# A decoder layer's output projection as seven block products, and transposes taken some turns later

## The chip, the cores and the metric

The kernel runs on one core of a Trainium2 chip. Its engines work side by side, each through its own list of instructions: TensorE (PE) multiplies matrices into PSUM banks, VectorE (DVE) and ScalarE (ACT) work elementwise, GpSimd (POOL) does a few small operations and issues DMA transfers that add into what is in memory, and SyncE (SP) issues the other DMA transfers. The metric is the device time of one execution in microseconds (us).

## The reference

One layer of a decoder on 512 tokens of width 1024, in float32. The part that matters here:

```python
x = x + (gate_r * ret_branch + gate_a * att_branch) @ w_o      # w_o: 1024 x 1024
u = rmsnorm(x, g_mlp) @ w_up                                   # w_up: 1024 x 4096
x = x + jnp.square(jax.nn.relu(u)) @ w_down                    # w_down: 4096 x 1024
gate_p = jax.nn.sigmoid(rmsnorm(x, g_ple) @ w_ple_gate)
return x + gate_p * (p_i @ w_ple_proj)
```

Ahead of it stand one input projection, a retention branch and an attention branch of three head groups. `gate_r` and `gate_a` are sigmoids of two column ranges of the input projection, and `ret_branch` and `att_branch` are each a product with a weight matrix.

## The kernel before

**Three products for one.** Every large matrix product keeps float32 accuracy by splitting both sides into a high and a low part in the matmul format (`fp32r`) and adding three products: high by high, high by low, low by high (`mm3`, lines 260 to 262). Weights come from HBM in units of 512 KB (`raw`, six buffers) and are split (`split_unit`): ScalarE copies the high part (`whi`, line 227), VectorE subtracts to get the low part (`wlo`, line 228), with four buffers each. `AHEAD` says how many units beyond the current ones are split in advance.

**Projections.** `rows_gemm` puts tokens on the output's rows: four banks of 128 tokens x 512 columns. `cols_gemm` puts output columns on the rows and all 512 tokens in the bank's columns.

**The mix of the branches (`mix`).** For each block of 256 output columns, and for the attention branch and then the retention branch, a `cols_gemm` makes the gate and another the branch product. VectorE multiplies the two (`gt`, line 899), GpSimd adds the branches (`gm`, line 905), ScalarE and VectorE split the sum into `mh` and `ml`. The blocks go in the order 0, 1, then 2, 3.

**The output projection (`tail`, first part).** The token rows `x` are loaded, and two `rows_gemm` calls (left and right 512 columns) multiply the 1024 merged columns by `w_o`. As each bank of 128 tokens finishes, VectorE adds it to `x` (line 1020), multiplies by the gain (line 383), and some turns later TensorE transposes the result (`pt`, line 336; `split_T`) into the left side of the next product, `h2`, which is split again (lines 349 and 350). ScalarE's squares of the row give its norm factor.

**The MLP.** It goes in four rounds of 1024 hidden columns. A round's up projection is eight `cols_gemm` calls. Its down projection is already done as seven block products instead of eight (`seven_gemm`): both sides are taken as 2 x 2 blocks (tokens by 256, columns by 512), sums and differences of blocks are formed, and seven products of them give the four output blocks. `seven_left` forms the left factors on VectorE and splits them (lines 932 to 940). The right factors are formed as the weights are loaded: `plan_seven` lists fourteen units, eight of which are a load on SP and then an accumulating load on POOL into the same buffer (line 196); two units are differences taken on VectorE (line 209). The products are traced in the order 4, 3, 5, 2, 1, 7, 6, and after each the accumulations into `x` (line 967), with `done` telling when an output block of 128 tokens x 512 columns is complete.

**What sets the order.** Work that is due later is put in a queue with a number of turns (`later`), and `tick` takes at most one ready item, the first in the list, at each turn; in a `rows_gemm` of 1024 columns a turn comes after every six matmuls. The head transposes (`heads_T`), the attention's value products and the transposes of normed rows get their place in TensorE's list this way. The planner of the language then orders each engine's list by its own estimate of when operands are ready, and hoists loads to where their buffers come free. Only in the last round's down projection and in the gate projection behind it do ScalarE and VectorE keep the order in which the program was traced (`manual_schedule`), with `AHEAD` 3 in that down projection.

In the last round `seven_gemm` calls `ready` for each complete block: the transposes for `h3` are put in the queue, and when a row has both halves its squares are traced at once (`mean_squares`, lines 391 to 394). The embedding rows `pp` (two loads of 1 MB) are traced ahead of that down projection. `big` is a pool of 16 buffers of 8 KB per partition, which holds `x1`, the left factors, `h2`, `h3`, `z` and `pp` among others.

Of the kernel before, what the change touches and what calls it, by code (L numbers as in the profile page):

```python
# [11 lines left out]
F32 = mybir.dt.float32  # L12
# [63 lines left out]
class Block:  # L76
# [504 lines left out]
    def att_proj(self, g, n):  # L581
# [24 lines left out]
        else:  # L606
            self.rows_gemm(self.hT, KD, consume)
        return self.heads_T(rots, g > 0, 12)

# [30 lines left out]
    def attention(self, g):  # L640
# [11 lines left out]
        def scores(r):  # L652
# [17 lines left out]
            for e in es:  # L670
                self.later(8, lambda e=e: pTs.append(self.transpose4(e)))
            self.later(13, lambda: values(r, wide, pTs), ("att", g, r))

# [105 lines left out]
    def ret_proj(self, extra=None):  # L779
        rots = []  # L780

        def consume(t, ps):
            z = self.tmp("rz")
            self.nc.scalar.activation(z, ps, AF.Copy, scale=self.r[:, t : t + 1])
            rots.append(self.rotate(z, self.rc[:, 1, t, :HD], self.rc[:, 1, t, HD:]))
            if extra is not None:
                extra(t, rots[t])

        self.rows_gemm(self.hT, KD, consume)
        return self.heads_T(rots, False, 7)  # L790

# [40 lines left out]
    def ret_head(self, h, qk, v, G, inner, A):  # L832
# [43 lines left out]
        for i in range(NT):  # L876
            self.later(2, lambda i=i: values(i))


    def mix(self, A, O):  # L880
        nc = self.nc
        mx = self.new_act(2, "m")
        self.spread_factors()
        for c in range(0, 4, 2):
            parts = {}
            for br, act, nk, bo in (("a", O, H, 24), ("r", A, KD, 16)):
                for cc in (c, c + 1):
                    sg = []
# [8 lines left out]
                    def branch(n, ps):  # L897
# [3 lines left out]
                        if br == "a":  # L901
                            parts[kk] = t
                            return
                        m = self.tmp("gm")
                        nc.gpsimd.tensor_tensor(m, t, parts[kk], op=ALU.add)
                        hi, lo = mx[0][kk // 4][:, kk % 4], mx[1][kk // 4][:, kk % 4]
                        nc.scalar.activation(R(hi), m, AF.Copy)
                        nc.vector.tensor_tensor(R(lo), m, hi, op=ALU.subtract)

# [7 lines left out]
                    self.cols_gemm(act, nk, branch)  # L917
        return mx

    def plan_mix(self):  # L920
        for c in range(0, 4, 2):
            for gate, w, nk in ((GA, self.a["w_att_out"][0], H), (GR, self.a["w_ret_out"][0], KD)):
                for cc in (c, c + 1):
                    self.plan_cols(self.w_in, gate + 256 * cc, KD)
                    self.plan_cols(w, 256 * cc, nk)
# [16 lines left out]
    def seven_gemm(self, U, xs, f, ready):  # L942
# [51 lines left out]
        for p in range(2):  # L994
            nc.vector.tensor_tensor(m4[p], m4[p], banks[1, p], op=ALU.add)
            acc(0, 0, p, m4[p])
            acc(1, 1, p, m4[p])
        for u in range(2):
            product(7, 5, u, False, u == 1)
# [10 lines left out]
    def tail(self, mx):  # L1010
        nc, a = self.nc, self.a
        xb = [self.big("x1") for _ in range(2)]
        xs = [xb[t // 2].rearrange("p (t c) n -> p t (c n)", t=2)[:, t % 2] for t in range(NT)]
        for t in range(NT):
            nc.sync.dma_start(xs[t], a["x"][0, t * P : (t + 1) * P])

        def add(half):
            def f(t, ps):
                v = xs[t][:, half * 512 : (half + 1) * 512]
                nc.vector.tensor_tensor(v, v, ps, op=ALU.add)  # L1020
            return f

        g2 = self.gain_row("g_mlp")
# [4 lines left out]

        def first(t, ps):
            add(0)(t, ps)  # L1030
            self.gain_T(xs[t], t, 0, g2, h2, "h2", 5)

        def last(t, ps):
            add(1)(t, ps)
            self.gain_T(xs[t], t, 1, g2, h2, "h2", 3)
            self.mean_squares(xs[t], v2[:, t : t + 1])

        self.rows_gemm(mx, KD, first)
        self.rows_gemm(mx, KD, last, group=4)
        nc.vector.reciprocal(f2[:, :NT], v2)  # L1040
        nc.vector.tensor_scalar(f2[:, NT:], f2[:, :NT], -1.0, None, op0=ALU.mult)

        h3 = None
        for f in range(NF // 2):
# [17 lines left out]
            for jj in range(2):  # L1062
                if f == 0 and jj == 0:
                    self.cols_gemm_halves(h2, KD, lambda n, ps: act(n // 2, n % 2, ps),
                                          lambda t: self.force(("h2", t, 1)))
                else:
                    for b in range(2):
                        self.cols_gemm(h2, KD, lambda n, ps: act(b, 2 * jj + n, ps))
            if f == NF // 2 - 1:
                pp = [self.big("pp") for _ in range(2)]  # L1070
                for half in range(2):
                    nc.sync.dma_start(pp[half], self.pp_dram[:, 512 * half : 512 * (half + 1)].rearrange(
                        "(t p) n -> p t n", p=P))
            ready = None
            if f == NF // 2 - 1:
# [3 lines left out]
                def ready(t, j, free):  # L1079
# [4 lines left out]
                    if halves[t] == 2:  # L1084
                        v = self.small(1, "v")
                        self.mean_squares(xs[t], v)
                        nc.gpsimd.tensor_tensor(r3[:, t : t + 1], v, self.mhalf[:, :1], op=ALU.pow)
            if f == NF // 2 - 1:
# [4 lines left out]

        self.AHEAD = 2
        out = self.a["out"][0]
# [15 lines left out]
    def make_plan(self):  # L1111
# [9 lines left out]
        self.plan_mix()  # L1121
        for half in range(2):
            self.plan_rows(a["w_o"][0], 512 * half, KD)
        for f in range(NF // 2):
# [50 lines left out]
```

## Time and profile before

| | us |
|---|---|
| median of 3 runs | 1014.93 (1014.62 to 1015.85) |
| the profiled execution | 1015.35 |
| its span | 1013.6 |
| output projection (first to last matmul) | 581.0 to 627.9 |
| four rounds of the MLP | 627.9 to 964.0 |
| weight loads of `w_o`, each | 512 KB, 3.3 from issue to landing |
| accumulating loads of `w_down`, each | 512 KB, 7.2 from issue to landing |

The span counts from the first to the last instruction that was recorded; the execution's own time is 1.75 us longer. In the profile's groups a line is that of the helper that issued the instruction, so tiles tell more than lines: `pg` and `pb` are product banks, `ph` a bank of head transposes, `pt` a bank of transposed rows, `hh` and `hl` the input's left side, `h2h` and `h2l` the MLP's, `h3h` and `h3l` the last gate's, `uh` and `ul` the left factors of the seven products, `raw` a weight unit as loaded. The ends of matmuls are modelled, so their starts are what is read. Durations of consecutive VectorE instructions overlap by up to 0.1 us.

### The profile page before, as it was taken

To read this page: it belongs to the slowest core of one execution; us is meant where nothing else is said; L and a number is where in the kernel's file an instruction comes from. 1 tells how busy PE (TensorE), PEld (TensorE's weight loads), DVE (VectorE), ACT (ScalarE), POOL (GpSimd) and SP (SyncE) were. 2 spreads that over 40 slices of the span, in tenths; PEclk is the share of its full clock that TensorE was granted. 3 is DMA by queue.
4 is the path that set the end of the run, shared out by engine and by line. 5 is a ranking of instruction groups with operands and counts; after the bars stand their busy time and mean duration, and the time that the engine had idled before them with its cause. 6 is when DMAs were issued, how large, how long until landed. Compare 5 with 4: busy or idle time off the path is not lost.

```text
span 1013.6 us, 12464 instructions
## 1 busy us (share of the span) xinstructions
PE 998.0 (98%) x4727; PEld 838.1 (83%) x4727; DVE 615.9 (61%) x895; ACT 455.1 (45%) x861; POOL 86.3 (9%) x92
## 2 busy tenths in 40 slices
PE   9899999999999999999999999999999999999898
PEld 6688889889887888888888888988888888888677
DVE  4787476566679444454543455478468559657763
ACT  7645444644533434333322324464454455455452
POOL 0110011011000000010100100100101001000100
PEclk9999999999999999999999999999999999999999
DMA  9634322233244421223324332559749757866711
GB/s 350 211 109 132 94 84 83 84 104 105 81 134 130 121 83 47 88 66 97 94 93 161 115 101 87 134 142 232 192 118 216 227 125 176 229 175 167 229 52 53
DMA packets 86492, 134.85 MB, mean 133 GB/s; under 512 B 6128, under 2 KB 38176, under 8 KB 86432
## 3 DMA queue, kind: packets, MB, share of 16 engines
q1 hardware_dynamic: 77584, 117.26, 36.0%
q0 software_dynamic: 8704, 16.78, 9.8%
q8 instruction: 37, 0.61, 0.2%
q14 instruction: 23, 0.19, 0.1%
q10 hardware_dynamic: 144, 0.02, 0.0%
HBM read 129.80 MB, written 4.24 MB: 132 GB/s over the span
## 4 chain that ended last, share of the span: by engine, by line
PE 89%; DVE 5%; DMA 3%; ACT 1%; issue 1%; SPq 0%; POOL 0%; ACTq 0%; DVEq 0%; POOLq 0%
PE pg L260 26%; PE pg L261 25%; PE pg L262 25%; PE pb L261 2%; PE pb L260 2%; PE pb L262 2%; PE po L683 1%; PE ph L560 1%; DMA raw<-in_w_in 1%; PE sc L660 1%; PE pt L336 1%; DMA raw<-in_w_down 1%; DVE wlo L228 1%; DMA x<-in_x 1%; PE ry L863 1%
## 5 line engine op out<-in xcount | busy, mean ns | idle before, releaser
L228 DVE TENSOR_TENSOR wlo<-raw,whi 128x1024 fp32r<-128x1024 f32 (+1 forms) x192 | 231.5, 1211 | 105.1 <-ACT whi L227 103.3
L227 ACT ACTIVATE whi<-raw 128x1024 fp32r<-128x1024 f32 (+1 forms) x192 | 197.4, 1032 | 204.5 <-PE pg L262 84.8
L260 PE MATMUL pg<-whi,hh 128*128 128x512 f32 x480 | 198.0, 414 | 0.0
L261 PE MATMUL pg<-wlo,hh 128*128 128x512 f32 x480 | 188.5, 393 | 0.1
L262 PE MATMUL pg<-whi,hl 128*128 128x512 f32 x480 | 188.5, 393 | 0.0
L262 PEld LDWEIGHTS pg<-whi,hl 128*128 128x128 f32 x480 | 98.2, 205 | 17.0
L261 PEld LDWEIGHTS pg<-wlo,hh 128*128 128x128 f32 x480 | 98.7, 206 | 14.9 <-DVE wlo L228 0.9
L260 PEld LDWEIGHTS pg<-whi,hh 128*128 128x128 f32 x480 | 98.4, 205 | 14.7 <-ACT whi L227 0.4
L261 PE MATMUL pg<-h2l,whi 128*128 128x512 f32 (+1 forms) x288 | 105.3, 366 | 0.0
L260 PE MATMUL pg<-h2h,whi 128*128 128x512 f32 (+1 forms) x288 | 105.2, 365 | 0.0
L262 PE MATMUL pg<-h2h,wlo 128*128 128x512 f32 (+1 forms) x288 | 105.2, 365 | 0.0
L326 POOL TENSOR_TENSOR r<-v,mhalf 128x4 f32<-128x4 f32 (+1 forms) x40 | 33.2, 830 | 395.7 <-DVE v L325 395.7
L196 POOL DMA_DIRECT2D raw<-in_w_down x32 | 38.8, 1221 | 321.0 <-DMA raw<-in_w_down 260.7
L260 PEld LDWEIGHTS pg<-h2h,whi 128*128 128x128 f32 x288 | 54.3, 189 | 8.8
L262 PEld LDWEIGHTS pg<-h2h,wlo 128*128 128x128 f32 x288 | 54.3, 189 | 8.7
L261 PEld LDWEIGHTS pg<-h2l,whi 128*128 128x128 f32 x288 | 54.3, 189 | 8.7
L260 PE MATMUL pg<-hh,whi 128*128 128x512 f32 x128 | 52.4, 409 | 0.0
L260 PE MATMUL pg<-whi,uh 128*128 128x512 f32 x128 | 50.1, 391 | 0.0
L262 PE MATMUL pg<-hh,wlo 128*128 128x512 f32 x128 | 50.0, 390 | 0.0
L262 PE MATMUL pg<-whi,ul 128*128 128x512 f32 x128 | 49.9, 390 | 0.0
L261 PE MATMUL pg<-hl,whi 128*128 128x512 f32 x128 | 49.9, 390 | 0.0
L261 PE MATMUL pg<-wlo,uh 128*128 128x512 f32 x128 | 49.8, 389 | 0.0
(190 smaller groups left out, 1659.3 us busy)
## 6 DMA issues: line engine op xcount, KB each, us to landing
raw<-in_w_in SPq DMA_DIRECT2D x72, 512.0 KB, 3.9
raw<-in_w_down SPq DMA_DIRECT2D x48, 512.0 KB, 4.1
raw<-in_w_up SPq DMA_DIRECT2D x32, 512.0 KB, 5.0
raw<-in_w_down POOLq DMA_DIRECT2D x32, 512.0 KB, 7.2
x<-in_x SPq DMA_DIRECT2D x8, 512.0 KB, 6.7
raw<-in_w_ret_out SPq DMA_DIRECT2D x8, 512.0 KB, 3.4
raw<-in_w_o SPq DMA_DIRECT2D x8, 512.0 KB, 3.3
raw<-in_w_ple_gate SPq DMA_DIRECT2D x8, 512.0 KB, 4.4
```

Source lines behind the costliest of these rows:

```text
L196: self.nc.gpsimd.dma_start(raw, rows(add[0]), accum_op=ALU.add)
L227: self.pin(nc.scalar.activation(R(hi[:, i]), raw[:, i], AF.Copy))
L228: nc.vector.tensor_tensor(R(lo[:, i]), raw[:, i], hi[:, i], op=ALU.subtract)
L260: t.matmul(ps, sh, mh, start=first, stop=False, skip_group_check=more)
L261: t.matmul(ps, sh, ml, start=False, stop=False, skip_group_check=more)
L262: t.matmul(ps, sl, mh, start=False, stop=last, skip_group_check=more)
L326: self.nc.gpsimd.tensor_tensor(r, v, self.mhalf[:, :w], op=ALU.pow)
L336: nc.tensor.transpose(ps[:, k * P : (k + 1) * P], part[:, k * P : (k + 1) * P], self.ident)
L560: self.nc.tensor.transpose(ps[:, t * P : (t + 1) * P], rots[t][:, h * HD : (h + 1) * HD], self.ident)
L660: nc.tensor.matmul(sc[:, h * P : (h + 1) * P], qT[:, h, rs], kT[:, h, rs], start=True, stop=True)
L683: nc.tensor.matmul(po[:, h * P : (h + 1) * P], v[:, vt, h * HD : (h + 1) * HD], pt, start=b == 0, stop=b == len(blocks) - 1)
L863: nc.tensor.matmul(y, sT[0][:, r], v[:, i, c], start=True, stop=i == 0)
```

## The change

The output projection becomes a call of `seven_gemm`, with ScalarE and VectorE in traced order, and `w_o` is planned with `plan_seven`. For that the mix makes left factors: the column blocks go in the order 0, 2, then 1, 3, so that column j and column j + 512 meet. For j below 512 GpSimd adds the branches as before and ScalarE copies the first 256 tokens into `z`; for the others VectorE adds straight into `z`, and `seven_left` follows. The loads of the token rows are traced within the mix, ahead of the second pair's retention branch. The transposes for `h2` are put in the queue as in the last round, and the squares three turns after. The factors from the norm are taken after the first round's up projection.

`AHEAD` is 3 in the output projection and goes to 2 inside every `seven_gemm` ahead of product 7. In the last round the squares are put in the queue (three turns) instead of being traced at once, and the loads of `pp` are traced behind the down projection. Three numbers of turns go up: the first query heads 12 to 16, the attention's value products 13 to 15, the retention's heads 7 to 9.

```diff
-        return self.heads_T(rots, g > 0, 12)
+        return self.heads_T(rots, g > 0, 16 if lazy else 12)
...
-            self.later(13, lambda: values(r, wide, pTs), ("att", g, r))
+            self.later(15, lambda: values(r, wide, pTs), ("att", g, r))
...
-        return self.heads_T(rots, False, 7)
+        return self.heads_T(rots, False, 9)
...
+    def load_x(self):
+        xb = [self.big("x1") for _ in range(2)]
+        self.xs = [xb[t // 2].rearrange("p (t c) n -> p t (c n)", t=2)[:, t % 2] for t in range(NT)]
+        for t in range(NT):
+            self.nc.sync.dma_start(self.xs[t], self.a["x"][0, t * P : (t + 1) * P])
...
-        for c in range(0, 4, 2):
+        for pair in ((0, 2), (1, 3)):
...
-                for cc in (c, c + 1):
+                if pair[0] and br == "r":
+                    self.load_x()
+                for cc in pair:
...
-                        m = self.tmp("gm")
-                        nc.gpsimd.tensor_tensor(m, t, parts[kk], op=ALU.add)
-                        hi, lo = mx[0][kk // 4][:, kk % 4], mx[1][kk // 4][:, kk % 4]
-                        nc.scalar.activation(R(hi), m, AF.Copy)
-                        nc.vector.tensor_tensor(R(lo), m, hi, op=ALU.subtract)
+                        j = kk % 4
+                        if kk < 4:
+                            m = self.tmp("gm")
+                            nc.gpsimd.tensor_tensor(m, t, parts[kk], op=ALU.add)
+                            z = self.big("z").rearrange("p a (b t) -> p (a b) t", b=2)
+                            nc.scalar.activation(z[:, 1], m[:, :256], AF.Copy)
+                            Z[j] = z, m[:, 256:]
+                        else:
+                            z, a21 = Z.pop(j)
+                            v = lambda ap: ap.rearrange("p (h t) -> p h t", h=2)
+                            nc.vector.tensor_tensor(z[:, 0:8:7], v(t), v(parts[kk]), op=ALU.add)
+                            for part, n in zip(U, ("uh", "ul")):
+                                part[j] = self.big(n)
+                            self.seven_left(z, a21, U, j)
...
+        self.AHEAD = 2
         for u in range(2):
             product(7, 5, u, False, u == 1)
...
-        self.rows_gemm(mx, KD, first)
-        self.rows_gemm(mx, KD, last, group=4)
-        nc.vector.reciprocal(f2[:, :NT], v2)
-        nc.vector.tensor_scalar(f2[:, NT:], f2[:, :NT], -1.0, None, op0=ALU.mult)
+        one = self.const.tile([P, 2 * NT], F32, name="one")
+        nc.gpsimd.memset(one[:, :NT], 1.0)
+        nc.gpsimd.memset(one[:, NT:], -1.0)
+        left = [2] * NT
+
+        def ready(t, j, free):
+            late = (t < 2) == (j == 0)
+            self.gain_T(xs[t], t, j, g2, h2, "h2", 0 if late else 1 + t // 2,
+                        None if late else (lambda s: free) if t < 2 else self.gbank)
+            left[t] -= 1
+            if not left[t]:
+                self.later(3, lambda: self.mean_squares(xs[t], v2[:, t : t + 1]), ("v2", t))
+
+        with self.tc.manual_schedule(engines={nc.scalar.engine, nc.vector.engine}):
+            self.AHEAD = 3
+            self.seven_gemm(mx, xs, one, ready)
...
-                                          lambda t: self.force(("h2", t, 1)))
+                                          lambda t: self.force(("h2", t, t // 2)))
...
-            if f == NF // 2 - 1:
-                pp = [self.big("pp") for _ in range(2)]
...
+            if f == 0:
+                for t in range(NT):
+                    self.force(("v2", t))
+                nc.vector.reciprocal(f2[:, :NT], v2)
+                nc.vector.tensor_scalar(f2[:, NT:], f2[:, :NT], -1.0, None, op0=ALU.mult)
...
                     if halves[t] == 2:
-                        v = self.small(1, "v")
-                        self.mean_squares(xs[t], v)
-                        nc.gpsimd.tensor_tensor(r3[:, t : t + 1], v, self.mhalf[:, :1], op=ALU.pow)
+                        self.later(3, lambda: factor(t))
...
-        self.AHEAD = 2
+        pp = [self.big("pp") for _ in range(2)]
+        for half in range(2):
+            nc.sync.dma_start(pp[half], self.pp_dram[:, 512 * half : 512 * (half + 1)].rearrange(
+                "(t p) n -> p t n", p=P))
...
-        for half in range(2):
-            self.plan_rows(a["w_o"][0], 512 * half, KD)
+        self.plan_seven(a["w_o"][0], 0)
```

More of the change, by code (lines that the diff above doesn't have):

```diff
@@ L877, in ret_head @@
             self.later(2, lambda i=i: values(i))
+    def load_x(self):
[3 more added lines that the diff above has]
+            self.nc.sync.dma_start(self.xs[t], self.a["x"][0, t * P : (t + 1) * P])
     def mix(self, A, O):
         nc = self.nc
-        mx = self.new_act(2, "m")
+        U, Z = [[None] * 4, [None] * 4], {}
         self.spread_factors()
-        for c in range(0, 4, 2):
+        for pair in ((0, 2), (1, 3)):
             parts = {}
             for br, act, nk, bo in (("a", O, H, 24), ("r", A, KD, 16)):
-                for cc in (c, c + 1):
+                if pair[0] and br == "r":
+                    self.load_x()
+                for cc in pair:
                     sg = []
@@ L917, in mix @@
                     self.cols_gemm(act, nk, branch)
-        return mx
+        return U
     def plan_mix(self):
-        for c in range(0, 4, 2):
+        for pair in ((0, 2), (1, 3)):
             for gate, w, nk in ((GA, self.a["w_att_out"][0], H), (GR, self.a["w_ret_out"][0], KD)):
-                for cc in (c, c + 1):
+                for cc in pair:
                     self.plan_cols(self.w_in, gate + 256 * cc, KD)
@@ L1011, in tail @@
         nc, a = self.nc, self.a
[L1012 to L1021, printed above, removed]
+        xs = self.xs
         g2 = self.gain_row("g_mlp")
@@ L1027, in tail @@
         r3 = self.const.tile([P, NT], F32, name="r3")
[L1029 to L1036, printed above, removed]
-        self.rows_gemm(mx, KD, first)
-        self.rows_gemm(mx, KD, last, group=4)
-        nc.vector.reciprocal(f2[:, :NT], v2)
-        nc.vector.tensor_scalar(f2[:, NT:], f2[:, :NT], -1.0, None, op0=ALU.mult)
+        one = self.const.tile([P, 2 * NT], F32, name="one")
[12 more added lines that the diff above has]
+            self.seven_gemm(mx, xs, one, ready)
         h3 = None
@@ L1068, in tail @@
                         self.cols_gemm(h2, KD, lambda n, ps: act(b, 2 * jj + n, ps))
-            if f == NF // 2 - 1:
-                pp = [self.big("pp") for _ in range(2)]
-                for half in range(2):
-                    nc.sync.dma_start(pp[half], self.pp_dram[:, 512 * half : 512 * (half + 1)].rearrange(
-                        "(t p) n -> p t n", p=P))
+            if f == 0:
[3 more added lines that the diff above has]
+                nc.vector.tensor_scalar(f2[:, NT:], f2[:, :NT], -1.0, None, op0=ALU.mult)
             ready = None
@@ L1084, in ready, with factor @@
                     if halves[t] == 2:
-                        v = self.small(1, "v")
-                        self.mean_squares(xs[t], v)
-                        nc.gpsimd.tensor_tensor(r3[:, t : t + 1], v, self.mhalf[:, :1], op=ALU.pow)
+                        self.later(3, lambda: factor(t))
+                def factor(t):
+                    v = self.small(1, "v")
+                    self.mean_squares(xs[t], v)
+                    nc.gpsimd.tensor_tensor(r3[:, t : t + 1], v, self.mhalf[:, :1], op=ALU.pow)
             if f == NF // 2 - 1:
@@ L1121, in make_plan @@
         self.plan_mix()
-        for half in range(2):
-            self.plan_rows(a["w_o"][0], 512 * half, KD)
+        self.plan_seven(a["w_o"][0], 0)
         for f in range(NF // 2):
```

## The prediction

> **What bounds the kernel now.** I read the page's busy times first, then the waits of TensorE alone, then stretches cut at the stage borders, and last the timeline inside the stages.
>
> ```profile
> PE 998.0 (98%) x4727; PEld 838.1 (83%) x4727; DVE 615.9 (61%) x895; ACT 455.1 (45%) x861; POOL 86.3 (9%) x92
> ...
> PE 89%; DVE 5%; DMA 3%; ACT 1%; issue 1%; SPq 0%; POOL 0%; ACTq 0%; DVEq 0%; POOLq 0%
> ```
>
> TensorE (PE) is busy 98% of the span and carries 89% of the chain that ended last. So a change is worth the TensorE work it removes plus the TensorE waits it removes, less the waits it makes. These are all the waits there are:
>
> ```profile
> PE ph L560 <- DVE ro L550: 4.3, 2, 3.5
> PE pt L336 <- DVE x L967: 2.9, 1, 2.9
> PE pg L260 <- ACT h3h L349: 1.6, 1, 1.6
> PE warm L429 <- DVE warm L425: 1.5, 1, 1.5
> PE po L683 <- DVE pT L149: 1.1, 1, 1.1
> ```
>
> Only 11.4 us, in five places: two at head transposes (3.5 and 0.8), one in an attention value product (1.1), two at the end of the last block product (2.9 and 1.6), one at the start, which the change leaves alone. Now the stretches: the output projection, the first and the last of the four seven-product stages that W_down has today, and five pieces around the waits.
>
> ```profile
> 581.02:627.89 46.87, 46.87 (x221) 38.77 (x220) 25.50 (x36) 16.74 (x28) 1.29 (x1) 1.00 0.25 71
> 673.23:711.30 38.07, 38.07 (x169) 31.53 (x168) 34.11 (x37) 18.51 (x19) 4.83 (x4) 1.00 0.79 199
> 918.02:964.02 46.00, 41.52 (x193) 33.47 (x191) 36.74 (x46) 23.05 (x34) 5.93 (x6) 1.00 0.76 217
> 45.00:48.30 3.30, 0.07 (x1) 0.07 (x2) 3.27 (x7) 0.00 (x0) 0.00 (x0) 1.00 0.00 0
> 48.30:53.00 4.70, 4.70 (x17) 3.79 (x18) 3.80 (x7) 1.18 (x2) 1.38 (x1) 0.64 0.62 167
> 924.00:952.00 28.00, 28.00 (x132) 22.84 (x131) 22.38 (x25) 11.61 (x15) 4.82 (x4) 1.00 1.03 282
> 952.00:956.00 4.00, 3.68 (x17) 2.71 (x15) 3.96 (x6) 2.29 (x3) 0.00 (x0) 1.00 0.38 135
> 956.00:960.00 4.00, 1.46 (x9) 1.30 (x10) 2.60 (x5) 1.34 (x4) 0.00 (x0) 1.00 0.49 149
> ```
>
> The columns after the length are TensorE, weight loads, VectorE (DVE), ScalarE (ACT) and POOL busy, then granted clock, DMA share and GB/s. Three things are to be seen. The projection has no idle TensorE time, so nothing but fewer matmuls shortens it. The same matrix product done as seven block products (168 matmuls of 128x512) took 38.07 us, 0.2266 us each, with no hole. And the same code under a fixed order of ScalarE and VectorE, with the results turned at once (the last stage), took 46.00.
>
> **The change part by part.** The sums stand against the profiled execution, 1015.35 us (span 1013.6 and 1.75 around it); the median shown, 1014.93, is 0.42 lower, and my time is the median less the sum.
>
> **1. Matmuls.** The projection has 4 x 8 x 2 x 3 = 192 matmuls today and 7 x 2 x 2 x 2 x 3 = 168 after: 24 x 0.2266 = **5.4 us** off TensorE. The eight groups of turns of the normed row stay; one costs
>
> ```profile
> 599.83 0.40 PE L262 MATMUL pg<-whi,ml 128*128 128x512 f32 x1
> 600.07 0.60 PE L336 MATMUL pt<-ident,y 128*128 128x128 f32 x4
> 600.42 0.48 PE L260 MATMUL pg<-whi,mh 128*128 128x512 f32 x1
> 600.73 0.39 PE L261 MATMUL pg<-wlo,mh 128*128 128x512 f32 x1
> ```
>
> 0.35 us plus 0.08 of the slower first matmul, 0.43. Of the eight, seven lie inside today's 46.87 us; after, six lie inside the stage and two (tokens 256 to 511, right half) behind it. If TensorE ran full the new stage would be 38.07 + 6 x 0.43 = 40.7 us, and the saving 46.87 - 40.7 - 0.43 = 5.7.
>
> **2. What the new stage puts on VectorE.** The first W_down stage keeps VectorE busy 34.1 of 38.07 us with splits of 14 weight units, two weight differences, the last left factor and the accumulations. The new stage has all that, and by these rows
>
> ```profile
> L899 DVE TENSOR_TENSOR gt<-gs,pg 128x512 f32<-128x512 f32 x16 | 11.0, 686 | 21.7 <-PE pg L262 21.7
> ...
> L383 DVE TENSOR_TENSOR y<-x,gr 128x512 f32<-128x512 f32 x8 | 5.5, 690 | 0.2
> ...
> L350 DVE TENSOR_TENSOR h2l<-pt,h2h 128x512 fp32r<-128x512 f32 x8 | 5.5, 688 | 4.7 <-ACT h2h L349 4.7
> ```
>
> a gate product and a merge add ahead of the last left factor, and before the stage's end six gain products and six low parts: 14 x 0.69 = 9.7 us, together **43.8 us**. That is over the 40.7 TensorE needs, so here VectorE becomes the limit, and in fixed order. First late is the fourth left factor: in the last stage its low part was done about 8.2 us after the stage began, exactly when TensorE came to it (36 matmuls, 8.2 us); with 1.4 us more ahead of it TensorE waits about 0.7 us. Late again are the turns of tokens 0 to 255, left half, which sit behind every split and accumulation before them. I take 44.5 us, 43.8 and that start, since in the stage without a wait the idle 4 us of VectorE lay where TensorE was ahead of it. Ends: 40.7 below; above, the last stage's 46.00 plus two gain products in its closing chain and the two additions, 4 x 0.69, so 48.8. Part 1 and 2 together: 46.87 - 44.5 - 0.43 = **-2.0** (-5.7 to +2.4). The projection's loads go from 8 to 12, and eight accumulating loads issued from POOL are new; the stretch has DMA share 0.25 today and the W_down stage lives with 0.79 without a wait, so they are at nothing unless the accumulating ones come late (rival C).
>
> **3. Mix.** Eight copies and eight low parts of the merged rows go, half of the merge adds leave POOL for VectorE, and four small copies and four left factors (four VectorE operations, one copy, one low part each) come in. They lie beside gate and branch products of 24 or 48 matmuls, 5.4 or 10.9 us, where ScalarE and VectorE have more than half of their time free; each product has a second pair of banks. Nothing, +1 if an evacuation queues behind a left factor. The token rows, four 512 KB loads, are issued some turns earlier on SP, ahead of the next weight loads; weights there are a unit or two ahead at share 0.25. Nothing.
>
> **4. End of the last stage.** This is why it lost time (VectorE's rows, then what SP and POOL issued):
>
> ```profile
> 949.44 1.23 DVE L228 TENSOR_TENSOR wlo<-raw,whi 128x1024 fp32r<-128x1024 f32 x1 [3.41 <-ACT whi L227]
> 950.58 0.69 DVE L350 TENSOR_TENSOR h3l<-pt,h3h 128x512 fp32r<-128x512 f32 x1
> 951.18 0.68 DVE L995 TENSOR_TENSOR m<-m,pb 128x512 f32<-128x512 f32 x1
> ...
> 955.28 1.22 DVE L228 TENSOR_TENSOR wlo<-raw,whi 128x1024 fp32r<-128x1024 f32 x1
> 956.41 1.41 DVE L233 SCALAR_TENSOR_TENSOR wlo<-raw,gcol,whi 128x512 fp32r<-128x512 f32 x2
> 957.74 0.75 DVE L967 SCALAR_TENSOR_TENSOR x<-pb,f,x 128x512 f32<-128x512 f32 x1
> ```
>
> ```profile
> 924.02 0.97 SPq L1072 DMA_DIRECT2D pp<-pp_dram  x2
> 932.59 1.54 SPq L194 DMA_DIRECT2D raw<-in_w_down  x2
> ```
>
> ```profile
> 940.48 1.20 POOL L196 DMA_DIRECT2D raw<-in_w_down  x1 [11.77 <-DVE h3l L350]
> 941.97 1.21 POOL L196 DMA_DIRECT2D raw<-in_w_down  x1 [0.29 <-DVE wlo L228]
> ```
>
> The two weight sums of product 6 came late: DMA was full (1.03) from 924 to 952, with 2 MB of embedding rows (pp) in front. VectorE stood 3.41 us for the first, then worked without a gap and reached the accumulation that the turns wait for only at 957.74. The change looks two units ahead instead of three from product 7 on, which takes the first gate split (956.41, two operations, 1.33 us) from ahead of it; it takes the squares from between token 0's and token 1's accumulation, and issues pp behind the stage. Without pp's move the accumulations would run at 956.4 and 957.1, the turns follow, 12 matmuls and two turns remain, and the stage ends near 960.6 instead of 964.02: -3.4. With pp out of the way it can reach 38.07 + 6 x 0.43 = 40.65 us, -5.35. But pp may be issued beside the accumulating loads at 940 to 950 and delay them there. Ends: 0, if they lose what the order gains, and -5.35. I take **-4.0**. The squares now lie under product 6 and the gate projection; uncovered they would cost four ScalarE operations a token.
>
> **5. Turns moved back.** The first query heads go from 12 to 16 turns of the queue, 5.4 us of matmuls later, against a wait of 3.5. After that wait the granted clock was 0.64 for 4.7 us, 1.7 us more: 5.2 in all. TensorE then comes to the next heads, the keys', 5.2 us sooner; their rows are
>
> ```profile
> 71.58 0.68 DVE L550 TENSOR_TENSOR ro<-ro,ro 128x512 f32<-128x512 f32 x1
> ...
> 73.18 0.60 PE L560 MATMUL ph<-ident,ro 128*128 128x128 f32 x4
> ```
>
> The last rotation ended 0.9 us before they began; at 68.0 it would be 4.3 us late if VectorE stayed as it is. VectorE is nearly full there but waits about 1.1 us for POOL's power at each token, and ScalarE, which stood behind the late heads, squares sooner. I take 2 us late: 5.2 - 2 = 3.2, rounded to **-3.0** (-5.2 to 0). The Trainium skill (TensorE: Matmul & The Clock Gate, "What's actually happening") has the array fall to half clock after an idle window of about 3.4 us. The trace agrees: 3.48 us idle gave 0.64, the 2.86 us before 958.5 left 1.00; by the rule a keys' wait under that length costs itself alone, a longer one the 1.7 us again.
>
> The value products go from 13 to 15 turns. In queue order the last block's second transpose then comes four turns ahead of its product rather than one: the wait of 1.1 goes, **-1.1** (0 if its copy stays behind VectorE's rotation). The retention heads go from 7 to 9. The queue is full of merge steps there, so they move by one turn, 1.36 us, against a wait of 0.8: **-0.7** (0 if VectorE, full there, slips as well). Later uses of all of these lie many turns behind.
>
> Sum: -2.0 - 4.0 - 3.0 - 1.1 - 0.7 = **-10.8 us**: 1004.5 against the profiled execution, 1004.1 as a median.
>
> **The rivals.**
> A, all stalls go: -5.7 - 5.35 - 5.2 - 1.1 - 0.8 = -18.2, 996.8; halfway between it and the forecast is 1000.5, and below that I count A. For it: the three W_down stages without a wait. Against: VectorE's 43.8 us in the new stage and the keys' rotation.
> B, the stalls move and do not go: the keys' heads wait as long as the queries' did (0), pp is issued into the accumulating loads and the end keeps all but the 1.33 us of the gate split, retention 0: -2.0 - 1.3 - 1.1 = -4.4, 1010.5. For it: VectorE is full in both places. Against: it has work in those stretches that nobody waits for.
> C, slower: in the new stage the weight sums land late and the fixed order makes every later accumulation and turn queue behind their splits, as in the last stage, where VectorE was idle 46.00 - 36.74 = 9.3 us. 43.8 + 9.3 = 53.1 us, which is 53.1 + 0.43 - 46.87 = +6.7; the last stage, in the same order, then gains nothing, and turns give -1.3 - 1.1 - 0.7: +3.6, 1018.5. It decides from a stage of 49.5 us on. For it: the order is the same. Against: there is no pp in that stretch. The Trainium skill (SBUF — State Buffer, "SBUF: two separate sides") speaks for it: a DMA issued from GpSimd cannot have its descriptors written while VectorE holds the port they share. The W_down stages have such loads with VectorE 90% busy and no wait of TensorE, so the trace doesn't show this at a price.
> D, no change: the new stage at its upper end, +2.4, the last stage and the first heads at nothing, -1.8 for the rest: +0.6, 1015.5. That it doesn't do what it says would be this one: a planner orders what isn't fixed, so a later turn need not come out later.
>
> **How the numbers follow.** Forecast 0.60, A 0.17, B 0.13, C 0.05, D 0.05. The forecast's own range is 1000.5 to 1008. The range for 8 in 10 takes A's upper part and B: 998.5 to 1010.5. Under 0.2% (2.0 us) a measurement of this kernel can't be told from no change; faster is the forecast, A and B, 0.90; same D, 0.05; slower C, 0.05.
>
> **What would show it.** A stretch of TensorE on the projection of 43 to 46 us with 168 matmuls, VectorE over 90% busy in it, and a wait of the turns (pt) or of the first half product (pg from h2) for VectorE. No wait at the first query heads, full clock from 48 to 53, but one of about 2 us at the keys' heads near 68. No wait at the value product near 124. The last stage at 41 to 43 us, with pp landing after the weight sums. I am wrong if the projection takes over 49 us, if the wait at the turns at the end is still near 3 us, or if a wait appears among the mix's products.

## The result, and the profile after

The changed kernel takes **1008.98 us** (median of 4 runs, 1008.86 to 1009.16) against 1014.77 for the kernel before (4 runs): a ratio of 0.9943 with a 95% interval of 0.9927 to 0.9959. It is 5.8 us faster. The forecast was 10.8 us faster, 1004.1; the time lies in the range of 998.5 to 1010.5, above the forecast's own range of 1000.5 to 1008, and nearer to rival B's 1010.5 than to the forecast. The profiled execution took 1008.86 us, its span is 1007.0 (before 1013.6).

The page's busy times, and then the waits of TensorE after the change (us in total, times, longest; two more rows have 0.2 us each):

```profile
PE 994.8 (99%) x4703; PEld 834.3 (83%) x4703; DVE 641.2 (64%) x929; ACT 465.3 (46%) x869; POOL 91.8 (9%) x98
...
PE 90%; DVE 4%; DMA 3%; issue 1%; ACT 1%; POOL 1%; SPq 0%; ACTq 0%; POOLq 0%; DVEq 0%
```

```profile
PE ph L560 <- DVE ro L550: 3.0, 2, 2.8
PE pg L260 <- ACT zn L591: 1.6, 2, 1.4
PE warm L429 <- DVE warm L425: 1.5, 1, 1.5
PE pg L260 <- ACT h2h L349: 0.7, 1, 0.7
PE pt L336 <- DVE y L383: 0.3, 1, 0.3
```

TensorE issues exactly the 24 matmuls fewer (4727 to 4703). Of the five waits of before, the two at the end of the last stage (2.9 and 1.6) and the value product's (1.1) are gone. The first line looks like before's 4.3, but it is another place: the **key heads** wait, not the queries'. And waits of 1.6 us in two, 1.4 the longest, for a bank behind ScalarE (`zn`) are new. The stretches, in the columns of the prediction's windows; four pieces of the front, the output projection, the first up projection behind it, the last block product:

```profile
40.00:50.00 10.00, 10.00 (x46) 8.29 (x45) 7.66 (x16) 4.85 (x17) 2.02 (x2) 1.00 0.51 163
50.00:58.00 8.00, 8.00 (x45) 6.64 (x44) 5.88 (x12) 4.54 (x14) 2.39 (x2) 1.00 0.60 192
58.00:74.00 16.00, 11.80 (x53) 9.22 (x53) 13.56 (x24) 6.52 (x19) 2.02 (x2) 1.00 0.23 66
74.00:84.00 10.00, 10.00 (x44) 8.17 (x45) 6.23 (x9) 3.90 (x5) 0.00 (x0) 0.83 0.35 107
581.64:624.41 42.77, 41.95 (x193) 33.46 (x191) 40.77 (x49) 18.41 (x22) 4.83 (x4) 1.00 0.68 172
624.41:671.19 46.78, 46.24 (x296) 42.09 (x297) 27.48 (x43) 29.48 (x50) 4.83 (x4) 1.00 0.63 158
915.99:957.13 41.14, 41.14 (x193) 33.75 (x192) 37.42 (x44) 21.88 (x29) 4.84 (x4) 1.00 0.84 243
```

The same four front pieces of before, for comparison:

```profile
40.00:50.00 10.00, 6.52 (x29) 5.14 (x28) 8.44 (x15) 3.90 (x12) 1.31 (x2) 0.95 0.55 188
50.00:58.00 8.00, 8.00 (x38) 6.59 (x37) 6.51 (x14) 3.75 (x12) 2.39 (x2) 0.85 0.49 157
58.00:74.00 16.00, 16.00 (x74) 13.30 (x73) 13.53 (x23) 7.68 (x24) 2.01 (x2) 1.00 0.29 81
74.00:84.00 10.00, 10.00 (x56) 8.38 (x55) 6.30 (x8) 4.30 (x6) 0.00 (x0) 1.00 0.44 128
```

From these rows and those of the prediction the 6.6 us between the spans are accounted for. The mix is cut at its first product of the retention branch (the first matmul that reads `A`):

| stretch | before | after | difference | forecast |
|---|---|---|---|---|
| start to the first product of the retention branch in the mix | 472.2 | 472.8 | +0.6 | -4.8 |
| from there to the output projection | 108.8 | 108.8 | 0 | 0 |
| output projection and the up projection behind it | 46.87 + 45.34 | 42.77 + 46.78 | -2.66 | -2.0 |
| from there to the last block product | 244.8 | 244.8 | 0 | 0 |
| last block product | 46.00 | 41.14 | -4.86 | -4.0 |
| behind it, to the end | 49.56 | 49.85 | +0.3 | 0 |

The two stages did a little more than forecast. **The front, which was to give 4.8 us, gave next to nothing**: the stall and the half clock of 40 to 58 us are gone, and 4.2 us of idle TensorE (16.00 less 11.80) and a clock of 0.83 stand at 58 to 84. Of the +0.6 a part is older than that: the first row that VectorE normalises (`zn`, line 597) starts at 30.22 us, before at 29.19. That start differs between profiles of one kernel (29.19 in e5 and 29.81 in e12 below, which have the whole change and one edit more), so this 1.0 us is not the change's, and without it the front gave about 0.4 us.

VectorE's and ScalarE's timeline there shows why:

```profile
61.82 0.69 DVE L550 TENSOR_TENSOR ro<-ro,ro 128x512 f32<-128x512 f32 x1
...
70.06 0.69 DVE L597 TENSOR_TENSOR zn<-zn,r 128x512 f32<-128x512 f32 x1 [1.19 <-POOL r L326]
70.79 0.69 DVE L545 TENSOR_TENSOR ro<-zn,C 128x512 f32<-128x512 f32 x1
71.40 0.75 DVE L548 TENSOR_TENSOR ro<-zn,S 128x256 f32<-128x256 f32 x2
72.07 1.22 DVE L228 TENSOR_TENSOR wlo<-raw,whi 128x1024 fp32r<-128x1024 f32 x1
73.21 0.68 DVE L550 TENSOR_TENSOR ro<-ro,ro 128x512 f32<-128x512 f32 x1
```

```profile
62.54 0.69 ACT L591 ACTIVATE zn<-pg,r 128x512 f32<-128x512 f32 x1 [2.82 <-DVE ro L550]
```

The last key rotation starts at 73.21; before it started at 71.58. TensorE got to the keys' heads earlier, at 70.68, and VectorE got there 1.6 us later, of which the late start is 1.0. ScalarE could not square sooner either: it stood 2.82 us because its evacuation `zn` takes a buffer that only the rotation at 61.82 gives back, and TensorE stood 1.4 us behind that for a bank.

### The profile page after: what moved, and what is told of

Read it like the earlier page. It is cut to its first block, busy times and chain, and to the rows that moved or that the text cites. A ratio compares the mean times of both kernels' runs of the same rounds, so it can differ in the third digit from the quotient of the medians.

```text
span 1007.0 us, 12493 instructions
## 1 busy us (share of the span) xinstructions
PE 994.8 (99%) x4703; PEld 834.3 (83%) x4703; DVE 641.2 (64%) x929; ACT 465.3 (46%) x869; POOL 91.8 (9%) x98
## 4 chain that ended last, share of the span: by engine, by line
PE 90%; DVE 4%; DMA 3%; issue 1%; ACT 1%; POOL 1%; SPq 0%; ACTq 0%; POOLq 0%; DVEq 0%
PE pg L260 25%; PE pg L261 25%; PE pg L262 25%; PE pb L260 3%; PE pb L261 3%; PE pb L262 3%; DMA raw<-in_w_in 2%; PE po L683 1%; PE ph L560 1%; PE pt L336 1%; PE sc L660 1%; PE ry L863 1%; PE pe L635 1%; POOL r L326 1%; DVE ro L548 1%
## 5 line engine op out<-in xcount | busy, mean ns | idle before, releaser
L227 ACT ACTIVATE whi<-raw 128x1024 fp32r<-128x1024 f32 (+1 forms) x198 | 203.4, 1033 | 199.6 <-PE pg L262 77.3
L228 DVE TENSOR_TENSOR wlo<-raw,whi 128x1024 fp32r<-128x1024 f32 (+1 forms) x198 | 235.8, 1195 | 89.4 <-ACT whi L227 87.9
L260 PE MATMUL pg<-whi,uh 128*128 128x512 f32 x160 | 62.7, 393 | 0.0
L262 PE MATMUL pg<-whi,ul 128*128 128x512 f32 x160 | 62.4, 391 | 0.0
L261 PE MATMUL pg<-wlo,uh 128*128 128x512 f32 x160 | 62.3, 390 | 0.0
L957 DVE TENSOR_TENSOR ul<-z,uh 128x1792 fp32r<-128x1792 f32 x20 | 40.5, 2026 | 15.9 <-ACT uh L956 15.9
```

Source lines behind the costliest of these rows:

```text
L227: self.pin(nc.scalar.activation(R(hi[:, i]), raw[:, i], AF.Copy))
L228: nc.vector.tensor_tensor(R(lo[:, i]), raw[:, i], hi[:, i], op=ALU.subtract)
L260: t.matmul(ps, sh, mh, start=first, stop=False, skip_group_check=more)
L261: t.matmul(ps, sh, ml, start=False, stop=False, skip_group_check=more)
L262: t.matmul(ps, sl, mh, start=False, stop=last, skip_group_check=more)
L957: nc.vector.tensor_tensor(R(lo), src, hi, op=ALU.subtract)
```

## The experiments

The first three take the change apart: each is the kernel before with one of its parts. M is the theory that the stall in the front moved to the keys' heads, V that VectorE's load sets the length of the new projection stage.

**e1_turns**: before, with the three turn numbers alone.

```diff
-        return self.heads_T(rots, g > 0, 12)
+        return self.heads_T(rots, g > 0, 16 if lazy else 12)
...
-            self.later(13, lambda: values(r, wide, pTs), ("att", g, r))
+            self.later(15, lambda: values(r, wide, pTs), ("att", g, r))
...
-        return self.heads_T(rots, False, 7)
+        return self.heads_T(rots, False, 9)
```

> The kernel before with only the three numbers of turns raised (12 to 16 for the first query heads, 13 to 15, 7 to 9). Theory M (the stall moves): the 3.5 us wait of the query heads and the half clock behind it come back as a wait of the key heads of about 3 us and a wait for a bank of about 1.6 us, with half clock again; the value products give 1.3 us; together 0 to 1 us faster than before. Theory R (what the prediction counted): 4.8 us faster, and the changed kernel's slow start (about 1 us in its first 40 us) hid a part of it.

Measured: 1014.49 against 1014.98 (ratio 0.9993, 0.9984 to 1.0001): no difference clear of the noise. Its waits and the piece behind the keys' heads:

```profile
PE ph L560 <- DVE ro L550: 3.0, 2, 2.8
...
PE pg L260 <- ACT zn L591: 1.5, 1, 1.5
```

```profile
58.00:74.00 16.00, 11.79 (x52) 9.31 (x51) 13.56 (x23) 6.06 (x16) 2.01 (x2) 0.97 0.23 67
74.00:84.00 10.00, 10.00 (x46) 8.07 (x46) 6.53 (x9) 4.44 (x6) 0.00 (x0) 0.88 0.36 112
```

The same waits as in the whole change, and the value product's wait is gone. So the front's null result comes from the turn numbers themselves and not from another part of the change.

**e2_proj**: before, with the new projection and the new order of the mix alone (turn numbers and last stage as before).

> The kernel before with only the output projection and the mix changed. Theory V (VectorE, in traced order, limits the new stage): the stage lasts about 42.8 us with VectorE over 90% busy and the up projection behind it about 1.4 us longer than before; 2.2 to 3.2 us faster than before. Rival (24 matmuls off TensorE count in full): 5.4 to 5.7 us faster.

Measured: 1014.06 (0.9989, 0.9980 to 0.9997). The projection's row is that of the whole change:

```profile
582.63:625.40 42.77, 41.96 (x193) 33.45 (x191) 40.73 (x48) 18.37 (x22) 4.83 (x4) 1.00 0.68 172
```

Its trace gains the same 2.6 us in the two stretches, as theory V says; the median shows 0.9 of it, with an interval of 0.3 to 2.0 us, less than the 2.2 expected. The profiled execution came to the mix 1.6 us later than before's, in code that is the same; the reason is with the next one.

**e3_last**: before, with the last block product's edits alone (`AHEAD` 2 from product 7 on, squares three turns later, `pp` traced behind).

> The kernel before with only the last stage's changes (two units ahead from product 7 on, squares three turns later, embedding rows loaded behind the stage). The last stage goes from 46.0 to about 41.1 us: 4.5 to 5 us faster than before, if what the trace shows there comes from these edits alone. Rival: under 2 us, if it needs the earlier parts of the change.

Measured: 1010.61 (0.9949, 0.9936 to 0.9963), 4.4 us by the medians and 3.8 to 6.5 by the interval, with the stage at 41.13 us: this part is most of the change. Its front is before's, and shows how uneven that is:

```profile
40.00:50.00 10.00, 6.55 (x30) 5.27 (x29) 7.66 (x16) 3.71 (x12) 2.01 (x2) 0.91 0.50 161
50.00:58.00 8.00, 8.00 (x32) 6.49 (x31) 6.27 (x13) 3.04 (x12) 1.38 (x1) 0.68 0.59 195
```

The clock's loss is (1 - 0.91) x 10 + (1 - 0.68) x 8 = 3.5 us here; by the rows of before above it is (1 - 0.95) x 10 + (1 - 0.85) x 8 = 1.7, after the same wait of 3.5 us. The price of 1.7 in my part 5 came from one execution, and from a cheap one.

The three medians together, -0.5 - 0.9 - 4.4 = -5.8, are the whole change. With intervals as wide as these, an agreement so close is partly chance; that the parts don't interact rests on the stages, which last the same alone as together (42.77 and 46.8 us in e2, 41.13 in e3).

**e4_first_heads_12**: after, with the first query heads back at 12 turns.

```diff
-        return self.heads_T(rots, g > 0, 16 if lazy else 12)
+        return self.heads_T(rots, g > 0, 12)
```

> The changed kernel with the first query heads back at 12 turns, all else as changed. Theory M: the wait of the query heads (3.5 us, half clock) returns and those of the key heads and of the bank go: within 1 us of the changed kernel, 1008 to 1010 us. Theory R: 3 to 5 us slower than the changed kernel, 1012 to 1014.

Measured: 1008.19 (0.9924, 0.9911 to 0.9936), no slower than with 16. The wait is where it was before (3.7 us in two, 3.5 the longest), the clock 0.85 and 0.76 over 40 to 50 and 50 to 58 us. Moving the query heads alone was worth nothing.

**e5_keys_16**: after, with the first group's key heads at 16 turns as well.

```diff
-        return self.heads_T(rots, g > 0, 16 if lazy else 12)
+        return self.heads_T(rots, g > 0, 16 if g == 0 else 12)
```

> The changed kernel with the first key heads also at 16 turns, 5.4 us of matmuls later. Theory M (the wait only moved from the query heads to the key heads, behind VectorE's rotations): the 3 us wait near 71 and the half clock behind it go, the 1.6 us wait for a bank near 61 stays; 3.5 to 5.5 us faster than the changed kernel, 1003.5 to 1005.5. Rival (VectorE is so full there that the wait moves on again, to the scores or the value projection): within 1 us of the changed kernel.

Measured: **1003.64** (1003.07 to 1004.55; 0.9884, 0.9871 to 0.9897). What is left of the waits in the front, and the two pieces:

```profile
PE pg L260 <- ACT zn L591: 1.1, 1, 1.1
...
PE ph L560 <- DVE ro L550: 0.2, 1, 0.2
```

```profile
58.00:74.00 16.00, 14.87 (x66) 11.99 (x65) 13.56 (x24) 6.25 (x15) 2.02 (x2) 1.00 0.25 72
74.00:84.00 10.00, 10.00 (x58) 8.43 (x57) 7.88 (x11) 5.38 (x7) 0.00 (x0) 1.00 0.79 248
```

VectorE does the same 13.56 us in 58 to 74 as before and after; TensorE has 66 matmuls there instead of 53, because it takes the next product's matmuls while VectorE catches up. The first product of the retention branch in the mix comes at 467.2 instead of 472.8, 1.0 of which is the earlier start. Theory M holds: with the keys' heads at 16 turns too, the move of the query heads pays. (The keys' heads alone at 16 turns were not tried.) The gain is 5.3 us against the changed kernel's median, 4.6 against e4 and 4.1 between the repeats below; part 5 had 5.2 for a stall that goes for good.

**e6_pp_ahead**: after, with `pp` traced ahead of the last block product again. **e8_order_back**: after, with `AHEAD` 3 through the last product and the squares at once; `pp` stays behind.

```diff
+            if f == NF // 2 - 1:
+                pp = [self.big("pp") for _ in range(2)]
...
-        pp = [self.big("pp") for _ in range(2)]
...
```

```diff
-        self.AHEAD = 2
+        if self.first:
+            self.AHEAD = 2
...
-                        self.later(3, lambda: factor(t))
+                        v = self.small(1, "v")
+                        self.mean_squares(xs[t], v)
...
```

> The changed kernel with the two 1 MB loads of embedding rows traced ahead of the last stage again. Theory P (the weight sums of product 6 came late because of these loads): they land near 30 and 34 us into the stage again instead of 24 and 30, and the last stage lasts 42.5 to 44 us instead of 41.1. Rival O (the order of splits and squares alone made the wait): it stays at 41.1.

> The changed kernel with three units ahead through the whole last stage and the squares traced at once, as before; the embedding rows stay behind the stage. Theory P: the stage lengthens only by what stands ahead of the turns, 0 to 1.5 us (41.1 to 42.6). Rival O: it is back near 45 us.

Measured: e6 1012.82 (0.9969, 0.9959 to 0.9980), e8 1011.13 (0.9955, 0.9943 to 0.9967). The stage in e6 and in e8:

```profile
916.34:962.28 45.94, 42.95 (x193) 34.87 (x192) 37.53 (x44) 21.77 (x29) 4.84 (x4) 0.96 0.76 217
```

```profile
917.08:959.58 42.50, 41.30 (x194) 33.57 (x192) 36.65 (x46) 23.14 (x34) 5.95 (x6) 1.00 0.81 235
```

The new order without the move of `pp` leaves the stage at 45.94, of which (1 - 0.96) x 45.94 = 1.8 us is the clock; the move without the order brings 42.50, both 41.14. (e6's profile is of the slowest of its eleven runs, which went from 1009.71 to 1014.15, and its stage is longer than either theory had.) So the move of the loads carries 3.5 of the 4.9 us by itself. What it does is seen in the loads between 900 and 970 us (KB each, median us from issue to landing), after and e6:

```profile
raw<-in_w_down POOLq DMA_DIRECT2D x5, 512.0 KB, 5.9
pp<-pp_dram SPq DMA_DIRECT2D x2, 1024.0 KB, 10.5
```

```profile
raw<-in_w_down POOLq DMA_DIRECT2D x5, 512.0 KB, 10.0
pp<-pp_dram SPq DMA_DIRECT2D x2, 1024.0 KB, 9.4
```

and in POOL's timeline, when the last two accumulating loads are issued, after and e6:

```profile
934.44 1.22 POOL L196 DMA_DIRECT2D raw<-in_w_down  x1 [7.87 <-DMA raw<-in_w_down]
937.30 1.21 POOL L196 DMA_DIRECT2D raw<-in_w_down  x1 [1.63 <-DVE wlo L228]
```

```profile
939.07 1.22 POOL L196 DMA_DIRECT2D raw<-in_w_down  x1 [12.01 <-DVE h3l L350]
940.56 1.21 POOL L196 DMA_DIRECT2D raw<-in_w_down  x1 [0.27 <-issue]
```

Without 2 MB of `pp` in front an accumulating load lands after 5.9 us instead of 10.0, and each is issued 3 to 4 us sooner in the stage. In e6 ScalarE stands for the weight sum and TensorE for the accumulation, as before the change (waits from 935 to 962 us):

```profile
ACT whi L227 <- DMA raw<-in_w_down: 3.5, 1, 3.5
...
PE pt L336 <- DVE x L984: 3.0, 1, 3.0
```

In e8 that last wait is gone, and one of 1.2 us of the gate product for `h3h` is left; it is what the order takes away.

**e7_no_gain**: after, with the gain product of the second norm left out (`None` for `g2`; the transposes take the rows themselves), so eight VectorE operations less in and behind the new stage.

```diff
-            self.gain_T(xs[t], t, j, g2, h2, "h2", 0 if late else 1 + t // 2,
+            self.gain_T(xs[t], t, j, None, h2, "h2", 0 if late else 1 + t // 2,
```

> The changed kernel without the product of the rows with the gain g_mlp (that product is left out, so the up projection works on rows without their gain): eight VectorE operations of 0.69 us fewer around the new stage. Theory V (VectorE in traced order limits the new stage): the stage of 42.8 us falls to about 41.3 and the up projection's stretch of 46.8 to about 46; 1.5 to 2.5 us faster than the changed kernel. Rival (accumulating loads or the turns themselves set it): under 0.5 us in these two stretches.

Measured: 1007.06 (0.9917, 0.9904 to 0.9930), and the two stretches:

```profile
582.11:623.61 41.50, 41.47 (x193) 33.67 (x192) 38.27 (x44) 20.53 (x25) 4.83 (x4) 1.00 0.72 190
623.61:669.37 45.76, 45.76 (x298) 41.92 (x296) 24.46 (x40) 27.37 (x47) 4.82 (x4) 1.00 0.59 150
```

42.77 + 46.78 becomes 41.50 + 45.76, 2.3 us less, and no idle TensorE is left in either. So VectorE is what the stage waits for, as theory V says, and 41.5 us is the stage with TensorE full; by my part 1 it was to be 40.7. Leaving the product out takes it from VectorE's load and also from the chain ahead of each group of turns; e7 can't tell these two apart, and the next two runs do so in part.

**e9_gain_pool** and **e11_two_on_pool**: e5 with four (two) of those eight gain products on GpSimd, which is nearly idle there (4.83 us of 42.77). Nothing is left out.

```diff
-            self.nc.vector.tensor_tensor(y, x[:, h * 512 : (h + 1) * 512], gain[h], op=ALU.mult)
+            eng = self.nc.gpsimd if lag else self.nc.vector
+            eng.tensor_tensor(y, x[:, h * 512 : (h + 1) * 512], gain[h], op=ALU.mult)
```

In e11 the condition is `lag == 2`, which holds for the left half of tokens 256 to 511.

> The kernel with both first heads at 16 turns, and of the new stage's eight gain products the four of the early fourths (token rows 0-255 right, 256-511 left) on GpSimd instead of VectorE. Nothing is left out. GpSimd's one operation of this shape in the trace (the sum of gated blocks, 128x512) took 1.64 us against VectorE's 0.63 us. Theory V (VectorE, 40.8 us busy of 42.8, is the limit of the new stage and of the stretch behind it): VectorE gives up 4 x 0.63 = 2.5 us, of which the kernel without any gain product showed the effect for eight: 87.26 us for the two stretches against 89.59. Half of that at least: the two stretches 88.0-88.6 us, time 1002.2-1003.0 against 1003.64. Rival P (GpSimd is too late): a product ends 1.0 us later and the transposes that have turn numbers of 1 and 2 wait for it; two stretches 89.6-91.0 us, time 1003.6-1005. Theory L (the late fourths decide, as their products stay on VectorE): 89.3-89.7 us, no change.

> As the kernel with four gain products on GpSimd, but with only the two of token rows 256-511 left on it; the two of rows 0-255 right, whose wait for GpSimd was 2.3 us, are VectorE's again. Nothing is left out. If VectorE's load sets the two stretches (theory V), it gives up 2 x 0.69 = 1.4 us and they come to 88.2-89.0 us against 89.59 with all on VectorE, 90.82 with four on GpSimd; time 1003.0-1003.6. If the latency of a product ahead of its transposes sets them (rival P: the wait of pt for GpSimd at 605 us, 0.64 us with four, stays), 89.5-90.3 us, time 1003.6-1004.6.

Measured: e9 1005.68 (0.9911, 0.9896 to 0.9926), slower than e5; e11 **1002.80** (1002.50 to 1003.79; 0.9880, 0.9862 to 0.9898). The stages in e9 and then in e11:

```profile
576.24:620.88 44.64, 42.09 (x193) 33.42 (x192) 42.80 (x45) 18.94 (x22) 9.95 (x8) 1.00 0.65 165
620.88:667.05 46.17, 45.98 (x297) 41.98 (x296) 26.93 (x43) 28.90 (x50) 4.81 (x4) 1.00 0.62 160
```

```profile
576.60:618.99 42.39, 42.00 (x194) 33.48 (x193) 40.34 (x47) 18.72 (x22) 7.36 (x6) 1.00 0.67 174
618.99:665.22 46.23, 46.14 (x298) 41.98 (x297) 27.16 (x43) 29.17 (x50) 4.82 (x4) 1.00 0.62 160
```

With four, TensorE waits for GpSimd (two waits, 2.3 us in total, at the first two products), and the two stretches grow to 90.8: the expectation's rival P, though the time is 0.7 us beyond even its range. The products took 1.3 to 2.1 us there, against 0.69 on VectorE. Nor did VectorE get lighter: it did four operations fewer and was busy 42.80 us instead of 40.77. These rows of e9 show where that went (the wait of TensorE first):

```profile
PE pb L336 <- POOL y L384: 2.3, 2, 2.0
```

```profile
596.51 4.93 DVE L228 TENSOR_TENSOR wlo<-raw,whi 128x1024 fp32r<-128x1024 f32 x1
```

```profile
596.09 1.75 POOL L384 TENSOR_TENSOR y<-x,gr 128x512 f32<-128x512 f32 x1
...
598.28 2.06 POOL L384 TENSOR_TENSOR y<-x,gr 128x512 f32<-128x512 f32 x1
```

A split that takes 1.22 us where GpSimd computes nothing took 4.93 beside GpSimd's first two products, and these took 1.75 and 2.06 us where each of e11's took 1.28. Side by side both engines were slower.

With two, the later ones, the sum is 88.6, 0.9 less than with none, and the wait of 0.7 us for `h2h` is gone. VectorE's busy time in the stage fell by 0.4 us only, not by the 1.4 of two products; one split beside them took 1.88 us. So a lighter VectorE counts where the operand isn't due, the latency where it is, and in both places GpSimd's work costs VectorE time as well.

**e10_after_again** (the changed kernel) ran beside e9, **e12_keys_16_again** (e5's kernel) beside e11.

> The changed kernel itself again, on the same chip as the kernel with four gain products on GpSimd. Expected that its time is settled, 1008.9-1009.2 us, and that the keys' wait at 70.9 us stands at 3.05 us in this profile too, with a clock of 0.83-0.89 between 74 and 84 us.

> The kernel with both first heads at 16 turns, on the same chip as the one with two gain products on GpSimd, so that the two differ by that alone. Stretches 42.8 and 46.8 us as in its first profile, 1003.2-1004.2 us; if the clock stays full in the front in this profile too (no wait of 2 us is left in it), the first A product starts within 0.5 us of 467.2 us; if the full clock was luck, up to 3.5 us later.

Measured: e10 1008.01 (1007.28 to 1009.49), e12 1003.87 (1003.23 to 1004.69). The changed kernel's time is less settled than its first four runs showed. The keys' wait stood again, at 2.7 us, but the expected fall of the clock did not come:

```profile
74.00:84.00 10.00, 10.00 (x52) 8.35 (x53) 7.34 (x10) 4.50 (x6) 0.00 (x0) 1.00 0.46 138
```

The first product of the retention branch came at 471.2 instead of 472.8 in this profile. In e12 it came at 467.8 (467.2 in e5), with a clock of 1.00 throughout the front and the difference of 0.6 there from the start (29.81 against 29.19): the full clock in e5 was no luck. e11 is 1.1 us under e12 on the same chip, its two stretches 88.6 against 89.5; the ranges of the runs still overlap, so the trace says it more firmly than the times. It is the fastest kernel found, 12.3 us under the kernel before.

## Why the prediction was right, and where not

The sign, the three waits that went and the two stages were right; the size was about half, and one step failed. That the time still lies in the range is partly luck: the two stages gave 1.5 us more than their terms, and without that it would have been about 1010.5, the edge.

**Part 5, the first heads, failed** (-3.0; about +1 in e1: 0.7 us off its span, of which the value product gives about 1.1, the last stage 0.5 and the retention heads 0.2; half of the +1 is a start 0.5 us later). The step was "I take 2 us late", between a bound of 4.3 "if VectorE stayed as it is" and 0. VectorE did stay as it was: 13.56 us of 16 against 13.53. My two reasons for the lower value did not hold: the rotation still waits 1.19 us for POOL's power (the row at 70.06), and ScalarE squares no sooner, since it waits for a buffer that the late rotation frees. The chain is closed: VectorE frees ScalarE's buffer, ScalarE's squares feed POOL, POOL's power feeds VectorE. Bringing TensorE forward does not speed it up. So the wait came in at 2.8 and one of 1.4 for a bank came with it, 4.2 together and so nearly the whole bound, and the clock fell again. That is rival B's mechanism (the keys wait as long as the queries did); B had 0 for this part. The keys' heads were 0.9 us from being late in the rows I had quoted and had the same 12 turns, so the change could have moved them too. e5 and e12 show the term's size when both are moved: 4.1 to 5.3.

**Part 5, the rest.** The value product's wait of 1.1 went, as forecast. The retention heads' wait fell from 0.8 to 0.2 us (the second of the two in the first line of the waits), but the stretch around it grew shorter by 0.2 only: the wait was mostly turned into other small gaps, which I did not follow further.

**Parts 1 and 2** (-2.0, measured -2.66). VectorE as the limit is shown by e7 and e11, and over 90% busy it was: 40.77 of 42.77 us, 95%. Mis-sized was its load, 43.8 by my count and 40.8 in the stage: all 14 added operations are there, but only 12 weight splits (line 228) where the first W_down stage has 14, which is 2.4 of the 3.0 us; and the fourth left factor cost no wait (0.7 forecast). The two waits named in advance came, the first half product's (0.7) and the turns' (0.3). The stretch behind grew by 1.44 where I had 0.43.

**Part 3** (0) was right: in both kernels the mix takes 40.3 us from its first product of the attention branch to the first of the retention branch, and 108.8 from there on. **Part 4** (-4.0, measured -4.86) was right in total and wrong in its shares: I gave the order 3.4 us without the move of `pp`, and feared that the move could give them back. e6 has 0.1 us for the order alone, 1.9 without the clock's loss in it; e8 has 3.5 for the move alone. With the last weight sums issued 3 to 4 us later, the order of what stands behind them matters little.

**Rival C** had a condition to decide on, a new stage of 49.5 us; it took 42.77, and TensorE waited nowhere for a weight sum. The Trainium skill's rule on the shared port (SBUF — State Buffer, "SBUF: two separate sides"), cited there, has no price in this stage: four of the eight accumulating loads went out in it, with VectorE 95% busy, and the other four in the mix. **Rival A**'s front needed e5's edit.

## What to carry to other kernels

When a stall at one consumer of a full engine is moved back, look at the next consumers of the same chain: bringing TensorE forward by the stall makes each of them late by as much, less the slack that the profile shows now (0.9 us here), unless the producer itself gets faster. Move all of them or none; together they gave 4.1 to 5.3 us here, the first alone nothing. Where transfers that are needed late stand ahead of transfers that are needed soon, try moving them first: here that was worth 3.5 us, and reordering the work that waits 0.1 to 1.9. And when work goes from VectorE to GpSimd, compare VectorE's durations beside it, not only its list: one split grew from 1.22 to 4.93 us here.

## What the runs showed of the hardware

After an idle stretch of TensorE the price of the clock is not a constant. Behind the same wait of 3.4 to 3.5 us it was 1.7 us in one profile (before) and 3.4 to 3.5 in three (e2, e3, e4). Behind the keys' wait of 2.7 to 2.8 us the granted clock of the next 10 us was 0.83 after the change, 0.88 in e1, 0.70 in e8 and 1.00 in e10, which is the same kernel as the changed one. And behind a wait of 3.0 us in e6's last stage the clock of the stage was 0.96, where before's 2.9 us left 1.00. The Trainium skill (TensorE: Matmul & The Clock Gate, "What's actually happening") has a window of about 3.4 us that runs freely. The spread between equal waits fits that; but a rule that a wait under 3.4 us costs only itself, which I had drawn from it, does not fit 0.83 behind 2.8 us. In this front another wait of 1.4 us stood 10 us before, and three head transposes stood directly ahead of the keys' wait; whether these count was not tried.

Behind the last block product every kernel with the new projection takes 0.3 us longer (49.82 to 49.90 against 49.56 to 49.63); its cause was not found.
